# Dealing one token tile by DMA instead of turning it on TensorE, and moving three scalings of the mixer from VectorE to ScalarE

## The chip, the cores and the metric

The kernel runs on one core of a Trainium2 chip. The metric is the device time of one execution in microseconds, and it is lower for a better kernel. In the rows of the profile PE is TensorE (matmuls), PEld its weight loads, DVE is VectorE, ACT is ScalarE, POOL is GpSimd and SP is SyncE, whose queue issues most of the DMAs.

## The reference

Two layers work on one sequence of 256 tokens, 1024 wide, in float32. What matters here is the first of a layer's four blocks and the beginning of the second:

```python
h = layer_norm(ALPHA * h + 0.5 * swiglu(h, ffn1_gate[l], ffn1_up[l], ffn1_down[l]), ln_g[l, 0], ln_b[l, 0])
z = h @ w_in[l]
cb, cc, ch, rq, rf, ri, rg, pu = jnp.split(z, split_at, axis=-1)
...
# hgrn2, the recurrent part of the mixer:
f = lb + (1.0 - lb) * jax.nn.sigmoid(f_logit)
logf = jnp.log(f)
k = 1.0 - f
...
o = o * lax.rsqrt(jnp.mean(jnp.square(o), axis=-1, keepdims=True) + RMS_EPS)
o = o * norm_g * jax.nn.sigmoid(g)
```

After the mixer come cross attention on a memory of 256 rows and a second feed-forward net (ffn2), each with its residual and layer norm.

## The kernel before

The 256 tokens are two tiles of 128: `h[0]` and `h[1]` hold the residual stream with a token on each partition. A product over the 1024 features needs the stream turned, with a feature on each partition: that is `xT`. Each float32 operand of a product is kept as a high part in fp32r and a low part (the rest), and a product is made of three: high by high, high by low, low by high. `split` makes the parts: ACT casts the source to the high part, DVE subtracts it from the source to get the low part. Weights stream from HBM by SP's queue into `raw` (three buffers), and are split into `whi` and `wlo` (eight buffers each).

The order is the program's order, rearranged for each engine by the tile framework's scheduler; only in some stretches (PE in the mixer's recurrence, DVE in the gate) is it written by hand. Every engine then works through its own list strictly in order.

The stretch around the change runs thus. `ffn(l, "ffn1", ...)` ends with `finish`: for token tile 0 and then tile 1 it makes the last products of the down projection (`tail`, two halves of 512 columns each), adds the residual (line 320), takes the statistics, and norms in two passes (lines 330 and 334). While PE still makes tile 1's last products, `transposed` turns the normed `h[0]` on PE: eight 128x128 transposes (line 170) into PSUM, from which `split` writes `xT`. `h[1]` is turned in the same way later: `finish` gives back a function for it, which the main loop puts into `keys(l, 0, {6: pend})`, ahead of the last of four column groups of the attention's keys. These groups read only the memory, so they fill PE while `h[1]` is normed. Then `mixer` begins. Its first products are the four column groups of f (its 512 columns from 1280 on), each of which reads `xT` of both token tiles.

In the mixer `ev_f` finishes f for two heads at a time: a sigmoid on ACT, then on DVE the scaling by `oml` and `lbs` (line 619) and k = 1 - f (line 623). `ev_g` does the gate's sigmoid on ACT and its scaling by the norm's gain on DVE (line 664).

In the nets, `turn` already brings a token-by-feature tile into feature-by-token form without PE: four DMAs on SP's queue deal rows of 32 (the tile `dealt`), a DVE transpose turns blocks of 32x32 (line 418, into `square`), and `split` makes the two parts.

Of the kernel before, what the change touches and what calls it, by code (L numbers as in the profile page):

```python
# [8 lines left out]
F32 = mybir.dt.float32  # L9
F32R = mybir.dt.float32r  # L10
U8 = mybir.dt.uint8
AF = mybir.ActivationFunctionType
ALU = mybir.AluOpType
# [4 lines left out]
P = 128  # L18
# [4 lines left out]
NT = SEQ // P  # L23
# [23 lines left out]
def model(ctx: ExitStack, tc: tile.TileContext, t: dict, out: bass.AP):  # L47
    nc = tc.nc
# [5 lines left out]
    def acc(shape=(P, 2, SEQ), tag="acc"):  # L54
        return ps.tile(list(shape), F32, tag=tag, name=tag)
# [4 lines left out]
    def split(hi, lo, src):  # L60
        nc.scalar.copy(hi, src)  # L61
        lows.append(nc.vector.tensor_tensor(lo, src, hi.bitcast(F32), op=ALU.subtract))  # L62
# [35 lines left out]
    def halves(a):  # L98
        return a.rearrange(
            "p (h c) -> p h c" if len(a.shape) == 2 else "p r (h c) -> p r h c", h=2  # L100
        )
# [7 lines left out]
    def sums(o):  # L109
        return o.rearrange("p (c h) -> p h c" if len(o.shape) == 2 else "p r (c h) -> p r h c", h=2)  # L110
# [19 lines left out]
    def mm_rows(o, xh, xl, wh, wl, start, stop):  # L130
        product(o, xh, wh, start, False)
        product(o, xh, wl, False, False)
        product(o, xl, wh, False, stop)

    def tok(i):
        return slice(i * P, (i + 1) * P)
# [5 lines left out]
    lbs = cst.tile([P, DEPTH, HEADS], F32, name="lbs")  # L142
    oml = cst.tile([P, DEPTH, HEADS], F32, name="oml")
    nhalf = cst.tile([P, 16], F32, name="nhalf")[:, 0:HEADS]
    h = [cst.tile([P, DM], F32, name=f"h{i}") for i in range(NT)]
# [16 lines left out]
    xTh, xTl = xT[:, :, 0, :], xT[:, :, 1, :]  # L162
# [4 lines left out]
    def transposed_half(src, i, j, dh, dl, unit=idn):  # L167
        pt = acc((P, 4, P))
        for k in range(4):
            nc.tensor.transpose(pt[:, k, :], src[:, (4 * j + k) * P : (4 * j + k + 1) * P], unit)  # L170
        split(dh[:, 4 * j : 4 * j + 4, tok(i)], dl[:, 4 * j : 4 * j + 4, tok(i)], pt)

    def transposed(src, i, dh, dl, unit=idn):
        for j in range(2):
            transposed_half(src, i, j, dh, dl, unit)
# [36 lines left out]
    ng = prm[:, 20:28].rearrange("p (l h) -> p l h", l=DEPTH)  # L212
# [76 lines left out]
        nc.sync.dma_start(b, t["ln_b"][l, n : n + 1, :].to_broadcast([P, DM]))  # L289
        return g, b  # L290

    def finish(mm, y, scale, gb, last=False, flip=False):

        g, b = gb
        for i in range(NT):
            st = sm.tile([P, 4, 6], F32, tag="st", name="st")  # L300
            pieces, size = [slice(0, 512), slice(512, DM)], 512
            if last and i == NT - 1:

                pieces, size = [slice(0, 512), slice(512, 768), slice(768, DM)], 256
                c = slice(512, DM)
                v = halves(h[i][:, c])
                nc.vector.scalar_tensor_tensor(v, v, ALPHA / scale, sums(y[i][1]), op0=ALU.mult, op1=ALU.add)
            for c in pieces:
                n = c.start // 512
                v = halves(h[i][:, c])  # L310
                if len(pieces) == 3 and n:
                    o = acc((P, 256))
                    mm(i, n, slice(c.start - 512, c.stop - 512), o, None)
                    nc.vector.tensor_tensor(v, v, sums(o), op=ALU.add)
                else:
                    mm(
                        i, n, slice(0, 512), None,
                        None if last or not i or not n else lambda: transposed(h[0], 0, xTh, xTl),
                    )
                    nc.vector.scalar_tensor_tensor(v, v, ALPHA / scale, sums(y[i][n]), op0=ALU.mult, op1=ALU.add)  # L320
                for d in range(c.start, c.stop, size):
                    nc.vector.bn_stats(st[:, d // size, :], h[i][:, d : d + size])
            mv = sm.tile([P, 2], F32, tag="mv", name="mv")
            nc.vector.bn_aggr(mv, st[:, 0 : DM // size, :])
            rs = sm.tile([P, 1], F32, tag="rs", name="rs")
            nc.vector.tensor_scalar_add(rs, mv[:, 1:2], LN_EPS / scale / scale)  # L326
            nc.gpsimd.tensor_tensor(rs, rs, nhalf[:, 0:1], op=ALU.pow)  # L327
            cs = [slice(0, 512), slice(512, DM)]
            for c in cs:
                nc.vector.scalar_tensor_tensor(  # L330
                    h[i][:, c], h[i][:, c], mv[:, 0:1], g[:, c], op0=ALU.subtract, op1=ALU.mult
                )
            for c in pieces:
                normed.append(nc.vector.scalar_tensor_tensor(
                    h[i][:, c], h[i][:, c], rs, b[:, c], op0=ALU.mult, op1=ALU.add
                ))
                if last:
                    e = nc.scalar if c.start == 512 else nc.sync
                    e.dma_start(out[0, tok(i), c], h[i][:, c])
        return lambda: transposed(h[1], 1, xTh, xTl, jdn if flip else idn)  # L340

    def project_back(slabs, late, gb, scale, between=lambda: None):
# [33 lines left out]
    def ffn(l, name, n, pend=None, last=False, early=None):  # L376
        gate, up, down = (t[f"{name}_{x}"][l] for x in ("gate", "up", "down"))
        with tc.tile_pool(name="ffn", bufs=2, reuse_waits="tile") as fp:
# [130 lines left out]
            def slab(c, u):  # L509
                if c < len(chunks) - 1:  # L510
                    w = load(down[c * CHUNK : (c + 1) * CHUNK], 2 * u, 2, 0, DM, strewn=True)
                else:
                    w = load(down, c * 4, 2, 0, DM)
                ah, al = acts[c]
                return w, ah[:, 2 * u : 2 * u + 2, :], al[:, 2 * u : 2 * u + 2, :]
# [4 lines left out]
            def rows_of(a, i, k, m, first, final, cols=slice(0, 512), alone=None):  # L520
                w, ah, al = a
                wh, wl = w.at(k, slice(m * 512 + cols.start, m * 512 + cols.stop))
                o = ys[i][m] if alone is None else alone
                mm_rows(o, ah[:, k, tok(i)], al[:, k, tok(i)], wh, wl, first, final)

            def both(c, u):
                a = slab(c, u)
                for i in range(NT):
                    for k in range(2):
                        for m in range(2):  # L530
                            apart = last and i == m == k == u == 1 and c == 3
                            rows_of(a, i, k, m, c == u == k == 0, apart)

            for c, (c0, ncol) in enumerate(chunks):
                if not c:
                    acts.append(first())
                    ys = [[acc((P, 512), "dn") for _ in range(2)] for _ in range(NT)]
                else:
                    acts.append(hidden(c0) if ncol == CHUNK else last_hidden(c0))
                if c == 1:  # L540

                    with tc.issue_after(loads[-1].ins) if early is not None else nullcontext():
                        gb = ln_params(l, n)
# [17 lines left out]
                        first = alone is not None and u == 0 and k == 0  # L561
                        rows_of(a, i, k, m, first, u == 2 and k == 1, cols, alone)

            return finish(tail, ys, 0.5, gb, last=last, flip=name == "ffn1")

# [24 lines left out]
    def mixer(l, fill):  # L592
        w_in = t["w_in"][l]
        with tc.tile_pool(name="mix", bufs=1, reuse_waits="tile") as mp:
# [10 lines left out]
            f = mp.tile([P, NT, HEADS, P], F32, tag="f", name="f")  # L605
            q = mp.tile([P, NT, HEADS, P], F32, tag="q", name="q")
            k = mp.tile([P, NT, HEADS, P], F32, name="k")
# [4 lines left out]
            square = mp.tile([P, NT, HEADS, 32], F32, name="square")  # L612
            AX_ = mp.tile([P, HEADS, P], F32, name="AX_")

            def ev_f(p):
                c = slice(2 * p, 2 * p + 2)
                nc.scalar.activation(f[:, :, c, :], f[:, :, c, :], AF.Sigmoid)
                for hh in (2 * p, 2 * p + 1):
                    nc.vector.tensor_scalar(
                        f[:, :, hh, :], f[:, :, hh, :], oml[:, l, hh : hh + 1], lbs[:, l, hh : hh + 1],  # L620
                        op0=ALU.mult, op1=ALU.add,
                    )
                nc.vector.tensor_scalar(
                    k[:, :, 2 * p : 2 * p + 2, :], f[:, :, 2 * p : 2 * p + 2, :], -1.0, 1.0,
                    op0=ALU.mult, op1=ALU.add,
                )

            for _ in columns(1280, 512, lambda j, o: add(f[:, :, j, :], o), ev_f, normed[-1].ins):
# [3 lines left out]
            gb = ln_params(l, 1)  # L632
# [28 lines left out]
            def ev_g(p):  # L661
                nc.scalar.activation(sg[:, 2 * p : 2 * p + 2, :], sg[:, 2 * p : 2 * p + 2, :], AF.Sigmoid)
                for hh in (2 * p, 2 * p + 1):
                    nc.vector.tensor_scalar_mul(sg[:, hh, :], sg[:, hh, :], ng[:, l, hh : hh + 1])

# [50 lines left out]
            def later(j, c):  # L718

                at = (j * 32 // c ^ 1) * c  # L720
                return slice(at, at + c)

            kc = blocks(1)
            for n, c in enumerate(LEVELS):
                a = 64 // c
# [4 lines left out]
                for hh in range(HEADS):  # L730
                    for j, g in enumerate(groups):
                        if c < 32:
                            x = view(qf, hh * P + 32 * j + c, (other - c, 2), (2 * c, 16 // c), (1, c))
                        else:
                            x = q[:, j * 32 // c % 2, hh, later(j, c)]
# [50 lines left out]
            sg = mp.tile([P, HEADS, SEQ], F32, tag="q", name="sg")  # L786
# [34 lines left out]
            with tc.manual_schedule(engines={E.DVE}):  # L821
# [3 lines left out]
                dealt = [scaled()]  # L825
# [7 lines left out]
            src = pu  # L833
            for g, w_ in enumerate(WINDOWS):
                d = pw[g % 2]
# [5 lines left out]
                pr, j = slice((g % 2) * 64, (g % 2) * 64 + 64), g // 2  # L841
                nc.vector.tensor_tensor(win[pr, j, 0:PAD], d[pr, j, PAD : 2 * PAD], invc[pr, j, :], op=ALU.mult)
                nc.scalar.mul(win[pr, j, PAD:], d[pr, j, 2 * PAD :], 1.0 / w_)
                src = d
# [4 lines left out]
            for j in range(2):  # L849
                nc.vector.tensor_scalar_mul(yc[:, j, :], u[:, j, 2 : 2 + SEQ], cw[:, l, 2, j : j + 1])  # L850
                for s in (1, 0):
                    nc.vector.scalar_tensor_tensor(
                        yc[:, j, :], u[:, j, s : s + SEQ], cw[:, l, s, j : j + 1], yc[:, j, :],
                        op0=ALU.mult, op1=ALU.add,
# [13 lines left out]
            for i in range(NT):  # L868
                y = yr[:, i]
# [159 lines left out]
```

## Time and profile before

| what | value |
|---|---|
| runs shown | 1093.29, 1093.42, 1093.48 us; median 1093.42 |
| the profiled execution's own time | 1093.2 us |
| its span, from the first to the last instruction | 1091.4 us |
| mean granted TensorE clock | 0.998 |
| busy: PE, DVE, ACT | 99%, 77%, 52% of the span |

The span is 1.8 us shorter than the profiled execution's own time, and that execution is 0.2 us below the median. Rows of a timeline give the start of a piece of work from the start of the span, its duration, the engine and line, the operation, the tile written and those read, and how many instructions are merged; a bracket at the end is the engine's idle time before it and what ended that. On DVE and ACT an instruction may start a little (0.1 us) before the one ahead of it ends, so steps from start to start are shorter than durations. In lists of waits the numbers are the total in us, the count, and the longest.

### The profile page before, as it was taken

The numbers are of one execution on the slowest core, as the hardware profiler recorded it, in microseconds if no ns is written. First come the engines' busy times: TensorE is split into PE (matmuls) and PEld (weight loads), VectorE is DVE, ScalarE is ACT, GpSimd is POOL, SyncE is SP. The second block draws the span as 40 slices with busy tenths as digits, with TensorE's granted clock in tenths as the row PEclk, the third lists the DMA queues.
The fourth block names the chain that finished last, engine by engine and source line by source line (L and its number), as shares of the span: only waits on it lengthen the run. The fifth ranks groups of instructions, "written<-read, shape, count | busy, mean of one in ns | idle before, by whom it ended". The sixth has DMA issues, their size and how long they took to land.

```text
span 1091.4 us, 15575 instructions
## 1 busy us (share of the span) xinstructions
PE 1079.9 (99%) x6051; PEld 953.4 (87%) x6051; DVE 836.9 (77%) x1091; ACT 571.7 (52%) x787; POOL 60.8 (6%) x113
## 2 busy tenths in 40 slices
PE   9999999999999999999999999999999999999997
PEld 7888888989898888888888888898898988888886
DVE  6678678998989867666687655789989888766665
ACT  6456454676556455444455445456664644544450
POOL 9500001000000000000000000010000000000000
PEclk9999999999999999999999999999999999999999
DMA  9986664745575487766488666646536664866651
GB/s 328 303 283 224 216 216 159 254 163 174 191 272 175 140 283 224 237 214 212 155 269 265 216 211 217 226 165 224 194 126 228 220 216 156 280 222 212 217 169 38
DMA packets 122665, 231.84 MB, mean 212 GB/s; under 512 B 6304, under 2 KB 45504, under 8 KB 117472
## 3 DMA queue, kind: packets, MB, share of 16 engines
q1 hardware_dynamic: 120800, 228.48, 63.2%
q0 software_dynamic: 1216, 1.20, 0.4%
q8 instruction: 47, 0.77, 0.3%
q10 hardware_dynamic: 576, 1.18, 0.3%
q14 instruction: 26, 0.21, 0.1%
HBM read 216.15 MB, written 1.05 MB: 199 GB/s over the span
## 4 chain that ended last, share of the span: by engine, by line
PE 93%; DVE 4%; ACT 1%; issue 1%; DMA 0%; DVEq 0%; ACTq 0%
PE acc L106 62%; PE dn L106 28%; PE acc L170 1%; DVE wlo L62 1%; DVE square L941 1%; PE dn L736 1%; DVE qTl L62 0%; PE dn L795 0%; DMA h<-in_x_dram 0%; ACT e L920 0%; DVE mx L913 0%; ACT L920 0%; DVE e L928 0%; DVE vl L62 0%; ACT whi L61 0%
## 5 line engine op out<-in xcount | busy, mean ns | idle before, releaser
L62 DVE TENSOR_TENSOR wlo<-raw,whi 128x1024 fp32r<-128x1024 f32 (+1 forms) x396 | 472.7, 1210 | 178.2 <-ACT whi L61 168.0
L61 ACT CAST whi<-raw 128x1024 fp32r<-128x1024 f32 (+1 forms) x396 | 402.1, 1041 | 334.5 <-PE dn L106 147.6
L106 PE MATMUL acc<-whi,xT 128*128 128x512 f32 x1312 | 394.9, 380 | 0.0
L106 PEld LDWEIGHTS acc<-whi,xT 128*128 128x128 f32 x1312 | 247.8, 189 | 35.3
L106 PE MATMUL acc<-wlo,xT 128*128 128x512 f32 x656 | 248.6, 379 | 0.0
L106 PE MATMUL acc<-xT,whi 128*128 128x512 f32 x576 | 142.1, 382 | 0.0
L106 PEld LDWEIGHTS acc<-wlo,xT 128*128 128x128 f32 x656 | 124.0, 189 | 17.3
L106 PE MATMUL dn<-whi,ah 128*128 128x512 f32 x346 | 131.5, 380 | 0.0
L106 PE MATMUL dn<-wlo,ah 128*128 128x512 f32 x346 | 131.1, 379 | 0.0
L106 PE MATMUL dn<-whi,al 128*128 128x512 f32 x346 | 131.1, 379 | 0.0
L106 PEld LDWEIGHTS acc<-xT,whi 128*128 128x128 f32 x576 | 104.1, 190 | 11.8
L106 PE MATMUL dn<-whi,xT 128*128 128x512 f32 x288 | 88.6, 382 | 0.1
L106 PEld LDWEIGHTS acc<-xT,wlo 128*128 128x128 f32 x576 | 75.5, 191 | 3.9
L106 PE MATMUL acc<-xT,wlo 128*128 128x256 f32 x576 | 75.9, 275 | 0.0
L106 PEld LDWEIGHTS dn<-whi,al 128*128 128x128 f32 x346 | 65.4, 189 | 9.3
L106 PEld LDWEIGHTS dn<-wlo,ah 128*128 128x128 f32 x346 | 65.4, 189 | 9.2
L106 PEld LDWEIGHTS dn<-whi,ah 128*128 128x128 f32 x346 | 65.4, 189 | 9.1
L418 DVE STREAM_TRANSPOSE square<-dealt 128x512 f32<-128x512 f32 x40 | 63.3, 1649 | 1.2 <-DMA dealt<-sg 1.2
L327 POOL TENSOR_TENSOR rs<-rs,nhalf 128x1 f32<-128x1 f32 x16 | 14.9, 929 | 857.5 <-DVE rs L326 857.5
L106 PEld LDWEIGHTS dn<-whi,xT 128*128 128x128 f32 x288 | 54.2, 189 | 8.7 <-DVE xT L62 1.0
L106 PE MATMUL dn<-wlo,xT 128*128 128x512 f32 x144 | 54.8, 380 | 0.3 <-DVE wlo L62 0.3
L320 DVE SCALAR_TENSOR_TENSOR h<-h,dn 128x512 f32<-128x512 f32 x31 | 21.1, 682 | 30.4 <-PE dn L106 30.4
(202 smaller groups left out, 967.4 us busy)
## 6 DMA issues: line engine op xcount, KB each, us to landing
raw<-in_ffn_up_dram SPq DMA_DIRECT2D x44, 1024.0 KB, 5.0
raw<-in_ffn_down_dram SPq DMA_DIRECT2D x44, 1024.0 KB, 5.1
raw<-in_ffn_gate_dram SPq DMA_DIRECT2D x42, 1024.0 KB, 5.0
raw<-in_w_in_dram SPq DMA_DIRECT2D x24, 1024.0 KB, 5.0
dealt<-sg SPq DMA_DIRECT2D x80, 128.0 KB, 3.2
raw<-in_ca_k_dram SPq DMA_DIRECT2D x8, 1024.0 KB, 4.9
raw<-in_w_out_dram SPq DMA_DIRECT2D x8, 1024.0 KB, 4.8
raw<-in_ca_v_dram SPq DMA_DIRECT2D x8, 1024.0 KB, 4.9
```

The source lines that it names most:

```text
L61: nc.scalar.copy(hi, src)
L62: lows.append(nc.vector.tensor_tensor(lo, src, hi.bitcast(F32), op=ALU.subtract))
L106: nc.tensor.matmul(o, w, x, start=start, stop=stop)
L170: nc.tensor.transpose(pt[:, k, :], src[:, (4 * j + k) * P : (4 * j + k + 1) * P], unit)
L320: nc.vector.scalar_tensor_tensor(v, v, ALPHA / scale, sums(y[i][n]), op0=ALU.mult, op1=ALU.add)
L327: nc.gpsimd.tensor_tensor(rs, rs, nhalf[:, 0:1], op=ALU.pow)
L418: nc.vector.transpose(d.rearrange("p k (i b) -> p b k i", b=4), x[:, :, i, :].rearrange("p b (j k) -> p b k j", k=4))
L736: nc.tensor.matmul(o[g, hh, :], kc[:, hh, g], x, start=True, stop=True)
L941: nc.vector.transpose(pt.rearrange("p m (i r b) -> p b (m i) r", i=2, b=4), pr[hh])
```

## The change

Two things are changed, in both layers.

First, behind ffn1's norm, `h[0]` is no longer turned on PE. `deal` copies each half of the normed tile on ACT into the free tile `z` in another order of columns, and issues four DMAs of 128 KB on SP's queue, which spread `z` over partitions. Behind the norm of `h[1]`, `dealt` turns each half with one DVE transpose of 32x32 blocks, and `split` writes `xT`; the split reads the turned tile in steps of 32 elements, since the blocks leave the tokens in another order. `h[1]` is turned on PE as before.

Second, in the mixer f's scaling, k = 1 - f, and the gate's scaling are made by ACT (Identity with scale and bias, and a multiplication by a column) instead of DVE.

```diff
-    def finish(mm, y, scale, gb, last=False, flip=False):
+    def finish(mm, y, scale, gb, last=False, flip=False, deal=None):
...
-                        None if last or not i or not n else lambda: transposed(h[0], 0, xTh, xTl),
+                        None if last or not i or not n or deal else lambda: transposed(h[0], 0, xTh, xTl),
...
+            if deal and not i:
+                dealt = deal(h[0])
+        if deal:
+            dealt()
         return lambda: transposed(h[1], 1, xTh, xTl, jdn if flip else idn)
...
+            def deal(src):
+                z = activations().rearrange("p i c -> p (i c)")
+                for j in range(2):
+                    nc.scalar.copy(
+                        z.rearrange("p (a k j) -> p k a j", a=4, j=32)[:, 4 * j : 4 * j + 4],
+                        src[:, 512 * j : 512 * j + 512].rearrange("p (k a j) -> p k a j", a=4, j=32),
+                    )
+                x = fp.tile([P, 4, NT, P], F32, tag="dealt", name="dealt", bufs=1)
+                for a in range(4):
+                    nc.sync.dma_start(x[a * 32 : a * 32 + 32], z[:, a * 256 : (a + 1) * 256])
+
+                def dealt():
+                    for j in range(2):
+                        d = fp.tile([P, 4, P], F32, tag="up", name="square")
+                        nc.vector.transpose(
+                            d.rearrange("p k (b r) -> p b k r", b=4), x[:, :, j, :].rearrange("p b (k j) -> p b k j", j=32)
+                        )
+                        split(
+                            *(w[:, 4 * j : 4 * j + 4, tok(0)].rearrange("p k (r b) -> p k r b", b=4) for w in (xTh, xTl)),
+                            d.rearrange("p k (b r) -> p k r b", b=4),
+                        )
+
+                return dealt
...
-            return finish(tail, ys, 0.5, gb, last=last, flip=name == "ffn1")
+            mixer_next = name == "ffn1"
+            return finish(tail, ys, 0.5, gb, last=last, flip=mixer_next, deal=deal if mixer_next else None)
...
-                    nc.vector.tensor_scalar(
-                        f[:, :, hh, :], f[:, :, hh, :], oml[:, l, hh : hh + 1], lbs[:, l, hh : hh + 1],
-                        op0=ALU.mult, op1=ALU.add,
+                    nc.scalar.activation(
+                        f[:, :, hh, :], f[:, :, hh, :], AF.Identity,
+                        bias=lbs[:, l, hh : hh + 1], scale=oml[:, l, hh : hh + 1],
                     )
-                nc.vector.tensor_scalar(
-                    k[:, :, 2 * p : 2 * p + 2, :], f[:, :, 2 * p : 2 * p + 2, :], -1.0, 1.0,
-                    op0=ALU.mult, op1=ALU.add,
+                nc.scalar.activation(
+                    k[:, :, 2 * p : 2 * p + 2, :], f[:, :, 2 * p : 2 * p + 2, :], AF.Identity, bias=1.0, scale=-1.0
                 )
...
-                    nc.vector.tensor_scalar_mul(sg[:, hh, :], sg[:, hh, :], ng[:, l, hh : hh + 1])
+                    nc.scalar.mul(sg[:, hh, :], sg[:, hh, :], ng[:, l, hh : hh + 1])
```

## The prediction

> **What bounds the kernel now.** I read the page's busy times first, then who PE (TensorE) waited for, then the busy time of each engine in the stretches that the change touches.
>
> ```profile
> PE 1079.9 (99%) x6051; PEld 953.4 (87%) x6051; DVE 836.9 (77%) x1091; ACT 571.7 (52%) x787; POOL 60.8 (6%) x113
> ```
>
> ```profile
> PE dn L437 <- DVE kTh L432: 1.5, 1, 1.5
> PE acc L106 <- ACT qTh L61: 1.1, 2, 0.5
> PE acc L106 <- DVE qTl L62: 0.7, 2, 0.3
> PE acc L170 <- DMA h<-in_x_dram: 0.5, 1, 0.5
> PE dn L106 <- DVE wlo L62: 0.3, 1, 0.3
> ```
>
> ```profile
> 176.50:192.00 15.50, 15.50 (x97) 14.16 (x96) 15.36 (x25) 10.73 (x16) 1.34 (x5) 1.00 0.53 177
> 191.90:212.80 20.90, 20.90 (x129) 19.21 (x128) 18.44 (x32) 15.02 (x23) 0.00 (x0) 1.00 0.81 274
> 715.00:730.50 15.50, 15.50 (x97) 14.17 (x96) 15.36 (x25) 10.67 (x16) 1.27 (x5) 1.00 0.50 168
> ```
>
> PE is busy for 99% of the span, and its waits come to 4.1 us, all at the start and in attention (qTh, qTl). In the stretch rows (PE, PEld, DVE, ACT, POOL, then the granted clock) PE runs without a break through the handover from ffn1 to the mixer, in both layers, and through the mixer's f and q products. So no wait is there to be removed: the change can gain only PE work that goes away. The same rows hold the danger: in the handover DVE is busy for 15.36 of 15.50 us. Whatever DVE is given there must show, unless something else leaves that stretch.
>
> **What goes.** Eight transposes of h[0] on PE, once a layer.
>
> ```profile
> 176.84 0.38 PE L106 MATMUL dn<-whi,al 128*128 128x512 f32 x1
> 177.05 1.04 PE L170 MATMUL acc<-idn,h 128*128 128x128 f32 x8
> 177.85 0.46 PE L106 MATMUL dn<-whi,ah 128*128 128x512 f32 x1
> 178.15 0.38 PE L106 MATMUL dn<-wlo,ah 128*128 128x512 f32 x1
> ...
> 188.38 1.04 PE L170 MATMUL acc<-jdn,h 128*128 128x128 f32 x8
> 189.17 1.76 PE L106 MATMUL acc<-mT,whi 128*128 128x512 f32 x7
> ...
> 191.88 1.67 PE L106 MATMUL acc<-xT,whi 128*128 128x512 f32 x7
> ```
>
> A product starts 0.215 us after the one before it (176.84 to 177.05). From 176.84 to 178.15 are 1.31 us with two such steps in them, so the transposes take 1.31 - 0.43 = 0.88 us. Two layers: 1.76 us, and with no wait anywhere that is the most that can be won: 1093.2 - 1.76 = 1091.4 for the profiled execution, 0.16%. A change of under 0.2% (2.2 us) is about what a measurement of this kernel can tell from none, so even the full gain is not "faster" by that bound.
>
> **What comes, step by step.** DVE's rows of the handover, then ACT's and SP's.
>
> ```profile
> 175.16 1.41 DVE L334 SCALAR_TENSOR_TENSOR h<-h,rs,lnb 128x512 f32<-128x512 f32 x2
> 176.49 0.68 DVE L320 SCALAR_TENSOR_TENSOR h<-h,dn 128x512 f32<-128x512 f32 x1
> ...
> 177.81 2.35 DVE L62 TENSOR_TENSOR wlo<-raw,whi 128x1024 fp32r<-128x1024 f32 x2
> 180.07 1.28 DVE L62 TENSOR_TENSOR xT<-acc,xT 128x512 fp32r<-128x512 f32 x2
> 181.27 0.68 DVE L320 SCALAR_TENSOR_TENSOR h<-h,dn 128x512 f32<-128x512 f32 x1
> ...
> 185.67 0.41 DVE L127 TENSOR_TENSOR sums<-acc,sums 128x256 f32<-128x256 f32 x1
> 186.00 1.21 DVE L62 TENSOR_TENSOR wlo<-raw,whi 128x1024 fp32r<-128x1024 f32 x1
> 187.14 0.41 DVE L127 TENSOR_TENSOR sums<-acc,sums 128x256 f32<-128x256 f32 x1
> ...
> 188.60 0.68 DVE L62 TENSOR_TENSOR kTl<-sums,kTh 128x512 fp32r<-128x512 f32 x1
> 189.21 1.21 DVE L62 TENSOR_TENSOR wlo<-raw,whi 128x1024 fp32r<-128x1024 f32 x1
> ...
> 190.68 1.27 DVE L62 TENSOR_TENSOR xT<-acc,xT 128x512 fp32r<-128x512 f32 x2
> 191.87 2.34 DVE L62 TENSOR_TENSOR wlo<-raw,whi 128x1024 fp32r<-128x1024 f32 x2
> ```
>
> ```profile
> 176.61 1.99 ACT L61 CAST whi<-raw 128x1024 fp32r<-128x1024 f32 x2 [11.25 <-PE dn L106]
> 206.95 0.85 ACT L712 COPY kc<-k 128x512 f32<-128x512 f32 x1 [1.40 <-DVE k L623]
> 221.24 0.62 ACT L712 COPY kc<-k 128x512 f32<-128x512 f32 x1 [0.51 <-DVE k L748]
> ```
>
> ```profile
> 139.22 2.61 SPq L415 DMA_DIRECT2D dealt<-sg  x4
> 166.64 13.91 SPq L76 DMA_DIRECT2D raw<-in_w_in_dram  x2
> ```
>
> ```profile
> dealt<-sg SPq DMA_DIRECT2D x80, 128.0 KB, 3.2
> ```
>
> The f products at 191.88 read xT of both token tiles. Before, the last thing they needed from DVE, the low parts of h[1]'s tile, ended at 190.68 + 1.27 = 191.95, the first half of them just ahead of the product: DVE and PE arrived together. The built program of the changed kernel gives DVE this order: the two wlo of 177.81; the residual of h[1] (L320) and its norm; a sum of keys; a wlo; the two new 32x32 transposes; the second sum; the low parts of the dealt tile; kTl; a wlo; the third sum; the low parts of h[1]; two more wlo with the fourth sum between them. So against before, two low parts leave 180.07 and stand later, two transposes are added, and one wlo goes from before h[1]'s low parts to behind them.
>
> ACT first. It copies each normed half of h[0] into z: the norm's two halves end at 175.87 and 176.57 (row 175.16), and ACT is idle, its casts waiting on PE until 176.61. At 0.62 each for a dense copy (row 221.24) the second copy ends at 177.2, and the cast that started at 176.61 starts then, 0.6 late. It takes about 1.04, so the wlo pair starts on DVE at 178.24 instead of 177.81, and the residual at 178.24 + 2.26 = 180.50. That is 0.77 ahead of before (181.27), since the two low parts of 1.2 no longer stand there; PE has h[1]'s sums 0.88 earlier, so it doesn't hold DVE up.
>
> SP next. Four issues took 2.61 (139.22), from 177.2 to 179.8; behind them in SP's queue is the third w_in load, issued before at 180.18 (the second of the two in row 166.64 starts 0.37 ahead of its end, 180.55) when the wlo pair had freed its buffer, and now not due before 180.6. It isn't held up. The last deal lands at about 179.2 + 3.2 = 182.4, and DVE comes to the first transpose at 186.4: four microseconds of cover. POOL's fill of AT is moved behind h[1]'s power; that lies beside all this.
>
> DVE from there, in steps from one start to the next (sum 0.33, wlo 1.13, kTl 0.61, a low part 0.60, all from the rows above): sum 184.90, wlo 185.23, first transpose 186.37. A transpose and the low parts behind it have no row of their own, so I bound them.
>
> ```profile
> L195 DVE STREAM_TRANSPOSE turned<-m 128x512 f32<-128x512 f32 x4 | 2.9, 721 | 0.0
> L418 DVE STREAM_TRANSPOSE square<-dealt 128x512 f32<-128x512 f32 x40 | 63.3, 1649 | 1.2 <-DMA dealt<-sg 1.2
> L748 DVE TENSOR_TENSOR k<-k,f 128x512 f32<-128x512 f32 x2 | 1.6, 788 | 0.0
> L62 DVE TENSOR_TENSOR xT<-acc,xT 128x512 fp32r<-128x512 f32 x40 | 25.9, 681 | 5.4 <-ACT xT L61 5.4
> L619 DVE TENSOR_SCALAR f<-f,oml,lbs 128x256 f32<-128x256 f32 x8 | 2.9, 409 | 1.4 <-ACT f L617 1.4
> L623 DVE TENSOR_SCALAR k<-f 128x512 f32<-128x512 f32 x4 | 1.7, 416 | 0.0
> ```
>
> The transpose lies between L195 (0.72, both sides in runs) and L418 (1.65, both sides in steps of four elements). The new one reads and writes runs of 32 elements, so I take L195: 0.65 from start to start. The steps have gone into the split behind it: ACT's cast and DVE's low part read the turned tile one element in 32. The nearest rows of such work are L748 at its first level (every second element: 0.79, against 0.68 dense) and kc at its first level (0.85 against 0.62); the upper end is what L418 pays over L195, 0.93 for two stepped sides. I take 0.88 for the low part and 0.85 for the cast.
>
> So: transposes 186.37 and 187.02, second sum 187.67, low parts at 188.00 and 188.80 (the casts end at 187.94 and 188.7), kTl 189.60, wlo 190.21, third sum 191.35, low parts of h[1] from 191.68, the first half done at 192.36. ACT's two casts of the dealt tile wait for the transposes and hold up kTh, h[1]'s casts and the third sum's copy behind them: 0.62 for kTh and as much for each of h[1]'s two take ACT to some 190.6, and DVE comes to h[1] at 191.68. Hand-overs between engines add some 0.2, an estimate: the f products start at 192.55. PE, which without its transposes would be there at 191.88 - 0.88 = 191.00, stands for 1.55 us. On the way PE's fourth key group needs the second sum's buffer: 188.1 against 189.17 - 0.88 = 188.29, no wait. Behind the start, the last wlo of the f weights ends at 195.7, where PE, with 11 whole products and six half ones done, asks for it at 195.6: 0.15 more. Later f and q work has slack of microseconds (DVE gets 4 x 0.41 + 2 x 0.42 = 2.5 us back from L619 and L623 in the f stage, where PE waits for nothing, so this covers but gains nothing). ACT takes that over: at 0.62 to 0.85 for a whole tile and at most the same for a half one, 3 to 5 us on 15.02 of 20.90; the gate's scaling (four halves a layer, from DVE to ACT) I cost at nothing too, since PE's list has no wait for the gate or the recurrence; without that cover it is 4 x 0.62 = 2.5 us a layer.
>
> The sum per layer: 192.55 - 191.88 + 0.15 = +0.8; two layers (the stretch from 715 shows the second as full as the first) +1.65. The profiled execution, 1093.2, becomes 1094.85; the median of the runs shown is 0.2 above it, so 1095.1, rounded to 1095.0: +0.15%, no change that would be told.
>
> **Rules weighed.** The Trainium skill, "VectorE: DVE Perf Modes", section "Rules for kernel authors", would turn a 128x128 tile on TensorE where PSUM will do as the place for the result, and that speaks against this change; by that advice the kernel stays at 0.88 us of PE a layer, against the 1.7 (1.55 + 0.15) of standing found above. The Trainium skill, "SBUF — State Buffer", section "Door 1: The DMA port swizzle", says that each access to a new 16-byte line pays a penalty, which is free up to a step of four float32; L748 pays 0.11 at a step of two, so the trace is harsher, and for a step of 32 the page gives no figure: its rule makes the rival that follows.
>
> **The rivals.**
> *The stepped reads cost as the stepped transposes do (slower).* If one stepped side costs half of L418's excess, 0.47, a low part takes 1.15 and a cast 1.09; the casts end at 188.18 and 189.2, the low parts run to 190.3, and everything behind is 0.7 later: +1.5 a layer, 1093.4 + 3.1 = 1096.5. If the transpose itself ran like L418, 0.87 each, it would be +2.6 a layer, 1098.5, and both 1100. It decides from 0.3 us a layer over my sum, 0.15 for each low part. For it: kc and L748 already pay at a step of two. Against: L195 shows runs to be cheap.
> *The cover is there after all (the full gain).* If DVE reached h[1]'s low parts 1.55 us sooner, PE would not stand: 1091.7. For it: DVE's order moves one wlo, 1.13, behind them. Against: 15.36 of 15.50; I found that wlo and still came late.
> *The deal comes late.* Past 186.4 each microsecond of landing is one of standing. Against: the last one, issued by 179.8, would have to take over 6 us to land, where 80 such deals took 3.2 under the same weight loads. 1 us late in both layers: 1097.
> *ACT becomes the bound in the mixer.* With 3 to 5 us more on 15.02 of 20.90, a late cast of q's or v's weights by 1 us a layer gives 1097. Against: PE needs them microseconds after ACT makes them.
> *The mixer's half does nothing.* That is in the forecast already.
>
> **How the numbers follow.** Chances: the forecast 0.43, the stepped reads 0.34, the cover (full or half) 0.13, a late deal 0.03, ACT 0.07. The forecast lies 0.6 us under the bound of 2.2, so part of it (0.03) crosses over: slower 0.42. The cover gives at most 1.76, so faster gets 0.04, for what I don't see. Same: 0.54. The range leaves out the dearest bounds: 1091.6 (the full gain) to 1098.8 (transposes like L418). The likeliest case's own range is 1093.6 to 1096.0.
>
> **What would show it.** Right: PE with a break of about 1.5 us just ahead of the first f product in each layer, put down to DVE xT; transposes of 0.72 at the new line; low parts of the dealt tile near 0.88; no waits of PE in the rest of the mixer. Wrong: no break there (then DVE's order or durations are off), a break ahead of the transposes put down to a DMA, or new waits for ACT between the f products and the recurrence.

## The result, and the profile after

| kernel | time, median (lowest to highest) | ratio to before, 95% interval |
|---|---|---|
| before, run beside it | 1093.48 us (1093.29 to 1094.09) | |
| after | 1097.65 us (1096.65 to 1099.33) | 1.0038 [1.0025, 1.0051] |

The change makes the kernel slower by 0.38%: little, but more than the 0.2% that a measurement tells from no change. The forecast was 1095.0, a change that could not be told from none. 1097.65 lies within the stated range, but above the likeliest case's own range (1093.6 to 1096.0), and the 4.2 us lost are beyond the bound of 2.2 us that the prediction drew for a change that can be told. The rival whose signs the profile shows is that of the stepped reads (1096.5). The profiled execution of after took 1096.65 us, the fastest of its five runs, with a span of 1094.9 us and a mean granted clock of 0.998.

Busy time on the page of after, and the head of PE's list of waits, the one row that is new in it:

```profile
PE 1079.6 (99%) x6035; PEld 952.6 (87%) x6035; DVE 836.3 (76%) x1075; ACT 585.0 (53%) x811; POOL 61.0 (6%) x113
```

```profile
PE acc L106 <- DVE xT L62: 4.0, 2, 2.0
```

PE has 16 instructions fewer, the 16 transposes, and stands twice for 2.0 us, once in each layer, for the low parts of `xT`. The stretches (PE, PEld, DVE, ACT, POOL, then the clock), and PE's timeline at the break in both layers:

```profile
176.50:192.00 15.50, 15.15 (x90) 13.54 (x88) 14.77 (x22) 11.66 (x17) 2.24 (x6) 1.00 0.54 171
191.90:212.80 20.90, 19.12 (x115) 17.43 (x116) 18.86 (x29) 16.75 (x27) 0.00 (x0) 1.00 0.75 252
```

```profile
188.00 1.04 PE L170 MATMUL acc<-jdn,h 128*128 128x128 f32 x8
...
191.27 0.38 PE L106 MATMUL acc<-mT,whi 128*128 128x512 f32 x1
193.68 1.75 PE L106 MATMUL acc<-xT,whi 128*128 128x512 f32 x7 [2.02 <-DVE xT L62]
...
728.02 1.04 PE L170 MATMUL acc<-jdn,h 128*128 128x128 f32 x8
...
733.69 1.53 PE L106 MATMUL acc<-xT,whi 128*128 128x512 f32 x6 [2.01 <-DVE xT L62]
```

In the second stretch PE, busy for all of 20.90 us before, loses 1.78; the clock is whole, so this is standing and not slowness. From the transposes of `h[1]` to the first f product are 5.68 us where before had 3.50 (188.38 to 191.88): 2.18 us of standing. The second layer shows the same, 5.67 us where before had 3.50 (726.93 to 730.43). Less the 0.88 us that the removed transposes gave, a layer is 1.30 us longer. What DVE, ACT and SP did meanwhile, in their timelines, and the groups of the new instructions (last number: idle time before them; the free tile `z` has the name `sg` in the rows):

```profile
178.69 2.36 DVE L62 TENSOR_TENSOR wlo<-raw,whi 128x1024 fp32r<-128x1024 f32 x2 [0.30 <-ACT whi L61]
180.97 0.68 DVE L320 SCALAR_TENSOR_TENSOR h<-h,dn 128x512 f32<-128x512 f32 x1
...
186.84 1.30 DVE L546 STREAM_TRANSPOSE square<-dealt 128x512 f32<-128x512 f32 x2
188.06 0.38 DVE L127 TENSOR_TENSOR sums<-acc,sums 128x256 f32<-128x256 f32 x1
188.73 2.13 DVE L62 TENSOR_TENSOR xT<-square,xT 128x512 fp32r<-128x512 f32 x2 [0.29 <-ACT xT L61]
190.75 0.71 DVE L62 TENSOR_TENSOR kTl<-sums,kTh 128x512 fp32r<-128x512 f32 x1
191.34 1.25 DVE L62 TENSOR_TENSOR wlo<-raw,whi 128x1024 fp32r<-128x1024 f32 x1
192.48 0.45 DVE L127 TENSOR_TENSOR sums<-acc,sums 128x256 f32<-128x256 f32 x1
192.81 1.31 DVE L62 TENSOR_TENSOR xT<-acc,xT 128x512 fp32r<-128x512 f32 x2
```

```profile
176.48 1.23 ACT L535 COPY sg<-h 128x512 f32<-128x512 f32 x2 [10.64 <-DVE h L334]
177.62 5.78 ACT L61 CAST whi<-raw 128x1024 fp32r<-128x1024 f32 x6
...
187.58 2.14 ACT L61 CAST xT<-square 128x512 fp32r<-128x512 f32 x2 [1.63 <-DVE square L546]
```

```profile
177.74 2.50 SPq L541 DMA_DIRECT2D dealt<-sg  x4
```

```profile
L546 DVE STREAM_TRANSPOSE square<-dealt 128x512 f32<-128x512 f32 x4 | 2.6, 687 | 0.0
L62 DVE TENSOR_TENSOR xT<-square,xT 128x512 fp32r<-128x512 f32 x4 | 4.3, 1095 | 0.6 <-ACT xT L61 0.6
L61 ACT CAST xT<-square 128x512 fp32r<-128x512 f32 x4 | 4.3, 1116 | 3.3 <-DVE square L546 3.3
L650 ACT ACTIVATE f<-f,lbs,oml 128x256 f32<-128x256 f32 x8 | 4.4, 594 | 0.0
L654 ACT ACTIVATE k<-f 128x512 f32<-128x512 f32 x4 | 2.5, 628 | 0.0
L694 ACT ACTIVATE sg<-sg,prm 128x256 f32<-128x256 f32 x8 | 3.6, 500 | 0.1
```

The transposes took 0.69 each and waited for no DMA. The split behind them is the dear part: 1.10 for a low part and 1.12 for a cast, against 0.68 and 0.62 for dense ones; DVE even waited 0.29 for the first cast. Everything behind stands that much later, down to the low parts of `h[1]`, which PE waits for.

### The profile page after: what moved, and what is told of

Same layout as the page of the kernel before. It is cut to its first block, busy times and chain, and to the rows that moved or that the text cites. A ratio compares the mean times of both kernels' runs of the same rounds, so it can differ in the third digit from the quotient of the medians.

```text
span 1094.9 us, 15563 instructions
## 1 busy us (share of the span) xinstructions
PE 1079.6 (99%) x6035; PEld 952.6 (87%) x6035; DVE 836.3 (76%) x1075; ACT 585.0 (53%) x811; POOL 61.0 (6%) x113
## 4 chain that ended last, share of the span: by engine, by line
PE 90%; DVE 7%; ACT 2%; issue 1%; DMA 0%; DVEq 0%; ACTq 0%
PE acc L106 60%; PE dn L106 27%; DVE wlo L62 2%; PE acc L170 1%; DVE square L971 1%; PE dn L766 1%; ACT xT L61 0%; DVE qTl L62 0%; DVE h L334 0%; ACT whi L61 0%; DMA h<-in_x_dram 0%; DVE h L330 0%; PE dn L825 0%; DVE xT L62 0%; DVE st L322 0%
```

## The experiments

Times of before beside these kernels were 1093.29 to 1093.46 us (medians of 9 to 21 runs).

**The two halves alone.** First the deal without the mixer's part: the three scalings go back to DVE.

```diff
-                    nc.scalar.activation(
-                        f[:, :, hh, :], f[:, :, hh, :], AF.Identity,
-                        bias=lbs[:, l, hh : hh + 1], scale=oml[:, l, hh : hh + 1],
+                    nc.vector.tensor_scalar(
+                        f[:, :, hh, :], f[:, :, hh, :], oml[:, l, hh : hh + 1], lbs[:, l, hh : hh + 1],
+                        op0=ALU.mult, op1=ALU.add,
...
```

> The deal of h[0] alone; f, 1 - f and the gate's scaling stay on DVE as before. If the loss is DVE's queue ahead of the first f product, the break of PE of 2.2 us stands there unchanged in both layers and the time is that of the whole change: 1096.5 to 1098. If ACT's new work in the mixer costs, the time falls by its share, to 1094 to 1095.5. If DVE's 2.5 us of scaling in the f stage matter once PE comes late, new waits of PE show in the f and q products and the time is above 1098.

Measured: 1097.98 us (1096.49 to 1099.65), ratio 1.0042 [1.0030, 1.0055]. Then the mixer's part without the deal: `finish` and `ffn` as before, the scalings on ACT.

> The mixer's scalings on ACT alone; h[0] is turned on PE as before. If PE waits for nothing in that stage, nothing is gained or lost: 1093.1 to 1093.8, with no new wait of PE. If ACT becomes a bound there: 1095 or more, with PE waiting for ACT in the f or q products.

Measured: 1093.37 us (1093.15 to 1093.74), ratio 1.0000 [0.9991, 1.0009]. So all of the loss is the deal's, and the mixer's half does nothing that can be told. Its f stage shows why, in the row of the same stretch as above:

```profile
191.90:212.80 20.90, 20.90 (x129) 19.20 (x128) 16.74 (x26) 17.39 (x29) 0.00 (x0) 1.00 0.69 239
```

DVE falls from 18.44 to 16.74 us and ACT rises from 15.02 to 17.39; PE is as full as it was.

**Where the spread comes from.** After's runs, and those of the deal alone, spread over some 3 us, where before's spread over 0.8 to 1.2. The profile of the deal alone caught the reason. PE's timeline, and then stretches of 3.41 us around its first break:

```profile
193.18 2.79 PE L106 MATMUL acc<-xT,whi 128*128 128x512 f32 x7 [1.99 <-DVE xT L62]
...
199.94 1.89 PE L106 MATMUL acc<-xT,whi 128*128 128x512 f32 x8
```

```profile
190.33:193.74 3.41, 1.42 (x10) 1.09 (x9) 3.41 (x7) 2.94 (x5) 0.10 (x1) 1.00 0.16 15
193.74:197.15 3.41, 3.41 (x13) 2.96 (x12) 3.41 (x5) 0.64 (x2) 0.00 (x0) 0.50 0.79 293
197.15:200.57 3.42, 3.42 (x22) 3.15 (x22) 2.28 (x3) 2.58 (x4) 0.00 (x0) 1.00 0.94 302
```

The same break as in after (1.99 us of idle time), but it is followed by one stretch of 3.41 us at half the clock, with 13 products where the next stretch has 22. The profile of after has breaks of the same size and no such stretch. The row of its PE timeline that matches the one of 199.94 comes first, then its stretches:

```profile
198.87 1.89 PE L106 MATMUL acc<-xT,whi 128*128 128x512 f32 x8
```

```profile
189.13:192.54 3.41, 2.52 (x16) 2.06 (x14) 3.41 (x5) 3.12 (x6) 0.10 (x1) 1.00 0.02 10
192.54:195.96 3.42, 2.28 (x14) 2.12 (x15) 3.42 (x7) 1.82 (x4) 0.00 (x0) 1.00 0.61 186
...
731.85:735.26 3.41, 1.57 (x7) 1.43 (x8) 3.41 (x6) 2.20 (x4) 0.00 (x0) 1.00 0.39 95
```

The same products take 6.76 us in the deal alone (193.18 to 199.94) and 5.19 in after (193.68 to 198.87), so the half-clock stretch cost 1.6 us. I laid these stretches on the same grid of 3.41 us, counted from the execution's first change of the clock (8.23 us in after, 6.00 in the deal alone). In after the first break falls across a boundary of the grid, so both of its stretches are two thirds to three quarters busy; in the second layer a stretch with 1.57 us of busy time still kept the clock, and the one with 1.42 lost it. The Trainium skill, "TensorE: Matmul & The Clock Gate", section "Part 1: The HAM clock gate", states a free-running window of 3413 ns and half rate after an idle window; the length and the grid agree with these rows. But the stretch need not be idle: here one that was 42% busy was enough. So a break of 2 us costs itself alone or 1.6 us more, by where it falls. The runs of the deal alone fit: 1096.49 us with a mean clock of 0.998, 1097.93, 1097.98 and 1098.09 with 0.996 or 0.997, and 1099.65 with 0.995. After's five fit more loosely: 1096.65 and 1096.86 us with 0.998, 1097.65 and 1097.87 with 0.997, 1099.33 with 0.995, and one half-clock stretch is worth 0.0016 of the mean. For the runs without a profile this is argued from their clocks, not shown.

**The price of the step.** The transposes write in steps of four elements, so that the turned tile is in order and the split reads and writes runs.

```diff
-                            d.rearrange("p k (b r) -> p b k r", b=4), x[:, :, j, :].rearrange("p b (k j) -> p b k j", j=32)
+                            d.rearrange("p k (r b) -> p b k r", b=4), x[:, :, j, :].rearrange("p b (k j) -> p b k j", j=32)
...
-                        split(
-                            *(w[:, 4 * j : 4 * j + 4, tok(0)].rearrange("p k (r b) -> p k r b", b=4) for w in (xTh, xTl)),
-                            d.rearrange("p k (b r) -> p k r b", b=4),
-                        )
+                        split(*(w[:, 4 * j : 4 * j + 4, tok(0)] for w in (xTh, xTl)), d)
```

> The whole change, with the steps moved back: the transposes write in steps of four elements and the split reads and writes whole runs. DVE's and ACT's orders are those of the change. If it is DVE's time in sum that counts, wherever the steps are paid: transposes of 1.2 to 1.4 us instead of 0.69, low parts of 0.68 instead of 1.1, casts of 0.62, and the f products start within 0.3 us of the change: 1096 to 1097.5. If the stepped casts on ACT are what delays, the time falls to 1095 or less. If a stepped transpose costs as those of the nets (1.65), 0.4 us later a layer: 1097.5 to 1098.5.

Measured: 1095.77 us (1095.51 to 1096.20), ratio 1.0021 [1.0012, 1.0030], between the first two times expected. The groups, and PE's waits:

```profile
L546 DVE STREAM_TRANSPOSE square<-dealt 128x512 f32<-128x512 f32 x4 | 4.5, 1226 | 0.0
L62 DVE TENSOR_TENSOR xT<-square,xT 128x512 fp32r<-128x512 f32 x4 | 2.6, 687 | 0.0
L61 ACT CAST xT<-square 128x512 fp32r<-128x512 f32 x4 | 2.5, 619 | 5.1 <-DVE square L546 5.1
```

```profile
PE acc L106 <- DVE xT L62: 2.1, 2, 1.1
...
PE acc L106 <- DVE sums L127: 0.8, 2, 0.4
```

The split is dense again, 0.69 and 0.62, and the transpose pays instead, 1.23 for 0.69. On DVE that is nearly even; what is won is the casts' half microsecond each. PE now stands 0.4 us at the fourth key group and 1.1 ahead of f, two short breaks for one long one, and the spread of the runs is gone: 0.7 us over eleven of them, all with a clock of 0.998 or 0.999. From the transposes of `h[1]` to the first f product are 5.34 us (187.96 to 193.30), 0.34 less than in after. That makes 0.7 us in two layers, as the profiled executions differ (1096.65 and 1095.99); the rest of the 1.9 us between the medians would be the half-clock stretches, which only after's runs have by their clocks.

The opposite: the split reads runs and writes `xT` in steps of four.

```diff
-                            *(w[:, 4 * j : 4 * j + 4, tok(0)].rearrange("p k (r b) -> p k r b", b=4) for w in (xTh, xTl)),
-                            d.rearrange("p k (b r) -> p k r b", b=4),
+                            *(w[:, 4 * j : 4 * j + 4, tok(0)].rearrange("p k (r b) -> p k b r", b=4) for w in (xTh, xTl)),
+                            d.rearrange("p k (b r) -> p k b r", b=4),
```

> The changed kernel with one thing altered: the split of the dealt tile reads the turned tile in runs and writes xT in steps of four elements, instead of reading one element in 32 and writing runs. Transposes and orders stay. Theory A (what was mis-sized is only the price of the stepped side, and a step of four costs what the second levels of k and kc cost or about half of the excess of the old deals' transposes): low parts of 0.8 to 0.95 and casts of 0.8 to 0.95 instead of 1.10 and 1.11, a PE break of 1.5 to 1.8 us a layer instead of 2.2, and 1095 to 1096.3, which is the time that the prediction's prices gave; no half-clock stretch. Rival (the price goes by whether there is a step at all, not by its width, or writes cost more than reads): low parts of 1.1 or more, a break of 2.2 or more, 1097 to 1099.

Measured: 1101.02 us (1099.82 to 1101.16), ratio 1.0068 [1.0055, 1.0080]: a miss, and past the rival too.

```profile
L62 DVE TENSOR_TENSOR xT<-square,xT 128x512 fp32r<-128x512 f32 x4 | 5.8, 1566 | 0.8 <-ACT xT L61 0.8
L61 ACT CAST xT<-square 128x512 fp32r<-128x512 f32 x4 | 5.3, 1438 | 3.3 <-DVE square L546 3.3
```

```profile
190.56:193.97 3.41, 0.60 (x5) 0.30 (x3) 3.41 (x6) 2.72 (x5) 0.10 (x1) 1.00 0.00 0
193.97:197.38 3.41, 3.33 (x8) 2.70 (x9) 3.41 (x5) 1.06 (x3) 0.00 (x0) 0.50 0.91 305
```

A step of four in what the split writes costs more than a step of 32 in what it reads: 1.57 for a low part, which also reads the high part in that step, and 1.44 for a cast, which only writes in it. So a narrower step was not a cheaper one; whether the side or the width makes it dear can't be told from these runs, which change both. The breaks grow to 2.9 us, and each is followed by a half-clock stretch.

**DVE's time, or only the step's?** If what counts is how long DVE is held, POOL could make the two low parts.

```diff
...
+                        nc.scalar.copy(hi, src_)
+                        nc.gpsimd.tensor_tensor(lo, src_, hi.bitcast(F32), op=ALU.subtract)
```

> The whole change, with the two low parts of the dealt tile made by POOL instead of DVE (2.1 us of DVE's queue a layer). DVE's order puts a wlo back ahead of h[1]'s low parts, and kTl still waits for ACT's two stepped casts, so if the loss is DVE's queue the f products start about 0.4 us sooner than in the change and the time is 1096 to 1097, provided that POOL makes a low part in under 2 us; every microsecond beyond that adds one a layer. If the stepped low parts themselves were the whole loss on top of the forecast, it would be 1095 or less.

Measured: 1102.86 us (1101.93 to 1103.54), ratio 1.0086 [1.0072, 1.0100], a miss by 6 us (POOL's 2.2 us for the first low part, 0.2 over the condition, would explain less than one). POOL's and DVE's timelines:

```profile
188.29 4.14 POOL L552 TENSOR_TENSOR xT<-square,xT 128x512 fp32r<-128x512 f32 x2 [4.91 <-ACT xT L551]
```

```profile
187.87 1.20 DVE L62 TENSOR_TENSOR wlo<-raw,whi 128x1024 fp32r<-128x1024 f32 x1
189.82 1.24 DVE L62 TENSOR_TENSOR kTl<-sums,kTh 128x512 fp32r<-128x512 f32 x1 [0.74 <-ACT kTh L61]
190.98 2.54 DVE L62 TENSOR_TENSOR wlo<-raw,whi 128x1024 fp32r<-128x1024 f32 x1
```

While POOL subtracts (188.29 to 192.43), a kTl of 0.67 takes 1.24 and a wlo of 1.21 takes 2.54. Not only is POOL slow (its 4.14 us for two may hold waits for DVE), it takes DVE's time as well. The Trainium skill, "SBUF — State Buffer", section "Who interferes with whom", says that a VectorE instruction with two inputs in SBUF and a GpSimd instruction that reads SBUF exclude each other for the whole of the one that came first; these rows agree with it. PE stood 3.4 us a layer and lost the clock behind both breaks, for two stretches of 3.41 us behind the first one and one behind the second. So whether DVE's queue or the step is what counts, this run can't say.

**Can the 0.88 us be had?** PE stands because its first f product needs a low part. So the loads of f were issued behind h[1]'s low parts, and PE was given the 28 high products of all four f groups first (with the dense split of the stepped transposes).

```diff
...
+            with tc.issue_after(turned_lows[-1].ins):
+                wf = load(w_in, 0, NK, 1280, 512)
+            of = [acc() for _ in range(4)]
+            with tc.manual_schedule(engines={E.PE}):
+                for j in range(4):
+                    for kk in range(NK - 1):
+                        product(of[j], wf.at(kk, tok(j))[0], xT[:, kk], kk == 0, False)
+                for j in range(4):
+                    for kk in range(NK):
+                        product(of[j][:, 0, :], wf.at(kk, tok(j))[1], xT[:, kk, 0, :], False, False)
+                    product(of[j], wf.at(NK - 1, tok(j))[0], xT[:, NK - 1], False, True)
...
```

> The deal kept, the transposes writing in steps of four so that the split reads runs, the four weight loads of f issued behind the low parts of h[1]'s tile, and PE making all 28 high products of the four f groups first, which read only the high parts, and the ones that read low parts behind them. Theory A (the standing ahead of f is DVE's time for low parts and wlo, and the gain of 0.88 us a layer is real once PE has work that doesn't wait for it): no break of over 0.3 us ahead of the first f product in either layer, so before less 0.88 to 0.9 a layer: 1091.7 (1091.4 to 1092.5), no half-clock stretch. Theory B (DVE is the bound of the whole handover, so the standing only moves to the first f product that reads a low part): the same total as the kernel with stepped transposes, 1095.8, with the break about 6 us later in the trace. Theory C (the new order itself costs on PE or on the loads): over 1094, and the control without the deal is slower than before by as much.

Measured: 1098.99 us (1098.50 to 1099.23), ratio 1.0049 [1.0036, 1.0061]. The control has the same order on the kernel before, with nothing dealt:

> Control: the kernel before, with nothing dealt, but with f's weight loads issued behind h[1]'s low parts and PE's f products in the order high ones first. Theory A and B: PE had no wait there to lose, so 1093.4 (1093.1 to 1093.7), nothing gained. Theory C (the order itself costs): 1094 or more. If the order itself brought something (say a wait in the f stage that I don't see), under 1092.9, and what the order brings beside the deal would have to be told apart from it.

Measured: 1095.86 us (1095.48 to 1096.57), ratio 1.0022 [1.0013, 1.0031]. Both missed theories A and B. The order, loads included, costs 2.4 us by itself, as theory C said; with the deal it is 5.5, not as much but more, and the deal alone with this split cost 2.3. PE's waits, first of the kernel with the deal, then of the control:

```profile
PE dn L777 <- DVE q L746: 3.1, 2, 1.6
PE acc L106 <- DVE f L127: 2.0, 2, 1.0
...
PE acc L106 <- DVE xT L62: 0.9, 2, 0.5
```

```profile
PE dn L750 <- DVE q L719: 0.9, 2, 0.5
...
PE dn L715 <- DVE q L127: 0.6, 2, 0.3
```

The wait ahead of f did fall, to 0.5 us a layer from 2.0 in after and 1.1 with the stepped transposes alone, and that is less than the 0.88 that was won: f starts 4.10 us behind the transposes of `h[1]` (187.59 to 191.69), 0.60 later than before. But PE then stands 1.0 for the sums of f and 1.6 in the recurrence for q, which DVE makes late. So theory B was right that the standing only moves, and wrong about the place (10 to 28 us later, not 6) and the total. Why DVE is late there, its timeline and the stretch around the wait for q show:

```profile
216.71 3.48 DVE L62 TENSOR_TENSOR wlo<-raw,whi 128x1024 fp32r<-128x1024 f32 x3
...
220.45 1.21 DVE L746 TENSOR_TENSOR q<-q,f 128x1024 f32<-128x1024 f32 x1
```

```profile
212.80:222.00 9.20, 7.69 (x122) 6.35 (x124) 9.20 (x12) 6.01 (x9) 0.00 (x0) 1.00 0.89 315
```

In the f stage DVE was not short of time: from 191.90 to 212.80 it was busy for 16.81 us of 20.90, less than before's 18.44, with idle time put down to ACT's casts and copies. From 212.80 to 222.00 it is busy throughout (8.26 of 9.20 us before), and three wlo stand ahead of q: the weights come later, and their low parts with them. Three variants took the order apart. With the stepped split of after, and otherwise as the first:

> The changed kernel as it is (the split reads one element in 32), with the loads of f issued behind h[1]'s low parts and PE's high products of f first. Theory A: DVE's first half of h[1]'s low parts is no longer needed by the first 28 products, but ACT's stepped casts (1.1 each) keep kTh and h[1]'s casts late, so a break of 0.3 to 0.8 a layer remains at the fourth key group or at the first f product: 1092.0 to 1093.5. Theory B (DVE's order only moves the standing): 1097 to 1098, as the changed kernel.

Measured: 1098.58 us (1098.42 to 1098.78), ratio 1.0046 [1.0033, 1.0058]: theory A missed, and theory B's time by 0.6 us. PE's waits are those of the first within 0.1 us, so the price of the split no longer shows. With the order of PE's products alone, the loads where they were:

> As the first one (dense split, PE's high products of f first), but with f's weight loads issued behind the norm, as in the changed kernel, so that two wlo stand ahead of the low parts of h[1] in DVE's order as before. Theory A in the form that what PE waits for is the last low part of h[1] alone: with the order of PE's products alone the wait is gone too, 1091.7 to 1092.5. Theory A in the form that the high parts of h[1] wait as well, since PE's buffer of sums comes free only when DVE has read it: a break of some 0.5 to 1.3 us a layer remains, 1093 to 1095.8.

Measured: 1096.36 us (1096.06 to 1096.71), ratio 1.0026 [1.0017, 1.0036]: the wait ahead of f is back (1.1 a layer in PE's waits), as the second form of theory A said, though the time is 0.6 us above its range, and the order costs 0.6 us against the same kernel without it. So of the 5.5 us some 2.3 are the deal with this split, 0.6 the order of PE's products and 2.6 the moved loads; PE's longest wait for q is 0.4 us here. With three groups first and the fourth whole behind them:

> As the kernel with all four f groups' high products first, but only the first three groups are made so, and the fourth stands behind them as a whole, as in the kernel before. If the loss of that order (2.4 us in the control without the deal) came from all four groups of f ending together, so that VectorE's and ScalarE's work for the recurrence piles up: the first pair of heads is done 1.1 us earlier than there, the wait for q in the recurrence falls from 3.1 us in both layers to under 1.5, the break ahead of f stays at 0.6, and a wait for the last wlo of up to 0.8 us a layer comes in: 1093 to 1095.5. If the loss came from the four weight loads moved behind the low parts (the recurrence's own loads later by as much): 1097 to 1099, as there. Under 1093.0 only if the wlo are in time.

Measured: 1097.77 us (1097.67 to 1098.40), ratio 1.0041 [1.0027, 1.0055]. That is 1.2 us less than with all four, and within the range that was given for the moved loads. PE's waits for q, 1.6 and 1.0 in both layers together, did not fall under 1.5; the wait for f's sums is gone, and one for the last wlo, 1.2, has come. No kernel tried here beats the one before.

## Why the prediction was right, and which size was off

The time came into the stated range, and the path was the one forecast: a break of PE just ahead of the first f product, put down to DVE's low parts of `xT`. But "no change that would be told" did not come true; the rival that the prediction held for second likeliest, 0.34, did. That the median is still inside the range is in part luck: the upper bound was drawn for dear transposes, which did not come, and some 0.7 us of the median belong to no term of the sum.

*What goes.* Right: 16 transposes fewer, and apart from 0.3 us in the first 10 us no other wait in PE's list changed. That the 0.88 us a layer is real shows in the kernel with PE's order changed, where f started only 0.60 us late; no kernel kept it to the end.

*ACT's copies, the wlo pair, the residual, SP.* Right. The profile of after runs 0.50 us late before the break (PE's transposes of h[1] at 188.00 for 188.38 - 0.88); the profile of the deal alone, with the same break, does not (its f starts at 193.18 for 193.68), so this is not the change's. It is there already at the start: the transposes that stand at 8.09 us in before and 8.12 in the deal alone stand at 8.58 in after, whose clock first changed at 8.23 where that of the deal alone did at 6.00. In after's time less 0.50 the pair starts at 178.19 (178.24 was forecast), the residual at 180.47 (180.50), the first transpose at 186.34 (186.37). The deals were issued by 180.2 and were not waited for. The rival of the late deal is out, with 2.8 to 3.4 us from issue to landing.

*The transposes.* Right: 0.69 each, the row taken was 0.72, so runs of 32 elements cost as runs do, and the bound by the old deals' transposes was out.

*The split behind them: the step that failed.* The low part was taken at 0.88 from the step of two elements, and measured 1.10; the cast was taken at 0.85 and measured 1.12. The longer cast also made DVE wait 0.29, which the sum didn't have. Followed through DVE's rows, less 0.50: the first low part at 188.23 (forecast 188.00), kTl at 190.25 (189.60), the third sum at 191.98 (191.35), the low parts of h[1] at 192.31 (191.68), the first f product at 193.18 (192.55). So 0.63 us a layer is lost in the split, and nothing behind it is off. It is the rival of the stepped reads: half of the old transposes' excess for one stepped side, 1.15 and 1.09, was the better price. It is a size that was off, taken from the mildest row at hand, and the mechanism stands.

*Behind the start.* Right: from the first f product the same products take 5.19 us where before took 5.02 (191.88 to 196.90), 0.17 more in each layer; 0.15 was forecast.

*The sum.* The forecast's +1.65, and 2 x 0.63 = 1.26, and 0.50 of the start make 3.41; the profiled executions differ by 1096.65 - 1093.2 = 3.45. The medians differ by 4.17, and those 0.7 us more are in no step of the prediction. By the clocks of the runs they are the half-clock stretches behind a break of 2 us; for after itself that is argued, not shown.

*The mixer's half.* Right: nothing, with 0.59, 0.63 and 0.50 us for ACT's new instructions and no new wait. The rival of ACT as the bound is out.

*The cover.* It did not come: PE stood 2.18 us a layer, and in the kernels with f's loads moved it still waited 0.4 to 0.5, and DVE's work came back later as waits for q.

## What to carry to other kernels

Where an engine is busy for 15.4 of 15.5 us, work that is moved onto it shows, unless as much leaves that stretch; and work that is put off to let it pass can come back as a wait at the next full stretch, as f's loads did at q. Find an engine with time to give before taking work from PE. When a layout is moved from one instruction into the next, price every instruction that inherits the step, on each engine, by the dearest row at hand rather than by the mildest; for stepped writes (1.57 and 1.44) even half of the dearest row's excess was too little. A break of PE need not cost only its own length: here breaks of 2.0 us cost the clock as well in some executions, and breaks of up to 1.6 us in none of the profiles.

## What the runs showed that had not been expected

- A break of 2.0 us lowered the granted clock to 0.50 for just one stretch of 3.41 us, in some executions and not in others; the stretch ahead of it had 1.42 us of PE's busy time in the one that lost the clock, and 1.57 in one that kept it. With the low parts on POOL, breaks of 3.4 us cost two such stretches in the first layer and one in the second.
- For float32 tiles of 128x512, one stepped side cost: reading one element in 32, 1.10 on DVE (0.69 dense) and 1.12 on ACT (0.62); writing in steps of four, 1.23 for the transpose (0.69), 1.44 for ACT's cast, and 1.57 for a low part that also reads one input so.
- A subtraction on POOL took about 2.1 us, perhaps with waits in it, and made a DVE subtraction beside it take 1.24 for 0.67, and 2.54 for 1.21.
